# A hybrid S5 / DeltaNet / attention block: the S5 output matrices of layer 0 made by DVE instead of GpSimd

## The chip, the cores and the metric

The kernel runs on one core of a Trainium2 chip. The metric is the device time in microseconds (us). Before the change the median of 3 runs is 2810.09 us (2808.03 to 2811.47). The engines are named as the profile names them: PE is TensorE (its weight loads are PEld), DVE is VectorE, ACT is ScalarE, POOL is GpSimd, and SP issues DMAs.

## The reference, cut to what matters

Two layers, 512 latent tokens and 256 context tokens of width 1024. Each layer normalises the tokens with adaLN shift and scale, multiplies them by one wide input projection `w_in`, runs three mixers side by side (a bidirectional S5 state space model, a chunked gated DeltaNet, windowed attention), merges them and ends with an MLP.

```
h   = rmsnorm(x, norm1_g) * (1 + sc1) + sh1          # sc1, sh1 = silu(c) @ w_mod + b_mod
u, dq, dk, dv, ..., aq, ak, av, gates = split(h @ w_in)
# S5, for each of two directions, 32 groups of 64 complex states:
s_t = a * s_{t-1} + bb @ u_t                         # a, bb from lam, log_dt, b
y_t = Re(c @ s_t) + d * u_t
```

The kernel works the S5 recurrence in chunks of eight tokens. For that it needs, per group and direction, the input matrices `bb * a^k` and the output matrices `c * a^k`, all complex. These products of powers are called tables here. They depend on weights alone, not on the tokens, and are made anew in every launch.

## The kernel before, in words

The program is written for a scheduler that puts each engine's instructions into an order of its own (from a modelled timeline). The order within an engine is then fixed: each engine works its queue strictly from the front, and waits there for what an instruction needs.

The first 350 us hold this work of layer 0:

- **adaLN.** 16 blocks of `w_mod` stream in (L250, issued by SP), PE multiplies them (L254), ACT copies (L257), PE turns the result (L260), DVE reduces and adds (L262, L264). The last L264 writes the last part of the modulation vector `modv`, the shift.
- **Norms.** DVE squares the tokens (L330), PE sums them, a few small steps on DVE and POOL (L345, L347) give the reciprocal root, and DVE multiplies it in (L380, tiles `ntl` for latent and `ntc` for context tokens, eight of each). The shift is added twice: ACT writes `hhi` (L389), the high part of the result, and DVE writes `hlo` (L390), the remainder. Both need the last `modv`.
- **Input projection.** For each weight block, ACT casts the high part `wh` (L230) and DVE makes the remainder `wl` (L231). PE multiplies in L180, over eight steps k, each three products (`hhi,wh`, `hlo,wh`, `hhi,wl`), 512 columns for latent and 256 for context tokens.
- **S5 tables** (`s5_tables`, L538). Layer 0 takes 4 rounds q of 4 group columns (NP=4); the round's two directions d follow one another. For each, DVE makes `tB` (L469 to L474) and from it `tX`, the input matrices. The output matrices `tC` are made from `tcc` and its negative `tcn` (L584 to L587). Both go through `cprod`:

```
u = [pool.tile([128, NP, 8, 16], F32, name=f"tu{nm}{i}", tag=f"tu{tg}{i}", bufs=1)[:, :, :n] for i in range(4)]
for k, (a, i) in enumerate(((src, 0), (src, 1), (src2, 1), (src2, 0))):
    v.tensor_tensor(u[k], a[:, i]..., pb[k % 2], op=OP.mult)      # L563, four
v.tensor_tensor(store(0), u[0], u[1], op=OP.subtract)             # L564
v.tensor_tensor(store(1), u[2], u[3], op=OP.add)                  # L565
```

  Here `v` is the engine, `tg` is "p" for POOL and "v" for DVE, and n is 7 for `tX` (448 columns an instruction) and 8 for `tC` (512 columns). Before, `v` is DVE for `tX` and POOL for `tC`. PE transposes `tX` (L599), ACT copies the result (L601), and it goes to memory in one DMA; PE multiplies `tC` by the padded `tB` (L609, tile `tz`) for the matrices `thx` (L616 to L620). `tC` goes to memory in four DMAs (L591).
- **S5 scan and rope.** On DVE, the scan of the chunk states (L729 to L732) stands between the steps of the rotary embedding for attention (L808, L810, L811, L852), whose result PE needs in L874.

From about 400 us on (DeltaNet, gates, merge, MLP, layer 1) the work is not touched. The tables of layer 1 are made by DVE already, one group column a round (NP=1, so 128 columns an instruction), in the MLP of layer 0.

The tables are a generator that other code drains: one step before the norms, four (`T0A = 4`) after the norms' statistics, which is all four rounds. So in program order all tables of layer 0 are written ahead of the gain and the shift; the scheduler spreads them from there.

Of the kernel before, what the change touches and what calls it, by code (L numbers as in the profile page):

```python
# [183 lines left out]
def setup(g):  # L184
    tc, nc, A = g.tc, g.nc, g.A
    es = g.es
    g.base = es.enter_context(tc.tile_pool(name="base", bufs=1))
    g.wp = es.enter_context(tc.tile_pool(name="wp", bufs=2))
    g.ps = es.enter_context(tc.tile_pool(name="ps", bufs=1, space=PSUM))
    g.dr = es.enter_context(tc.tile_pool(name="dr", bufs=1, space=DRAM))  # L190
    g.ca = g.base.tile([128, CA_N], F32, name="ca")
    nc.sync.dma_start(g.ca, A["ca"])
    g.sm = g.base.tile([128, SM_N], F32, name="sm")
    nc.sync.dma_start(g.sm, A["small"])
    g.ident = g.ca[:, CA_ID:CA_ID + 128]
    g.ones = g.base.tile([128, 32], F32, name="ones")
    nc.gpsimd.memset(g.ones, 1.0)
    g.cneg = g.base.tile([128, 1], F32, name="cneg")
    nc.gpsimd.memset(g.cneg, -0.5)
    g.cpos = g.base.tile([128, 1], F32, name="cpos")  # L200
    nc.gpsimd.memset(g.cpos, 0.5)
    g.hpi = g.base.tile([128, 1], F32, name="hpi")
    nc.gpsimd.memset(g.hpi, math.pi / 2)
    g.modv = g.base.tile([128, NL, 48, 2], F32, name="modv")
    nc.gpsimd.memset(g.modv[:, 1, :, 1], 0.0)
    g.g1 = g.base.tile([128, 8, 2], F32, name="g1a")
    g.g2 = g.base.tile([128, 8, 2], F32, name="g2a")
# [27 lines left out]
def cond_setup(g):  # L235
    nc = g.nc
    c = g.p5a[1].tile([128, 8, NCH], F32, name="cond", tag="uy", bufs=2)[:, :, :32]
    nc.sync.dma_start(c, g.A["cond"])
    g.cs = g.base.tile([128, 8, 32], F32, name="conds")
    nc.scalar.activation(g.cs, c, AF.Tanh, scale=0.5)  # L240
    nc.vector.scalar_tensor_tensor(g.cs, g.cs, 1.0, c, op0=OP.add, op1=OP.mult)


def adaln(g, l, nbs, pool, bufs=2):
    nc = g.nc
    for nb in nbs:
        ps = pm(g, "s")
        for kp in range(4):
            w = pool.tile([128, 1024], F32, name="wa", tag="wa", bufs=bufs)
            g.ad_last = nc.sync.dma_start(w, g.A["wmod"][nb, kp])  # L250
            for k2 in range(2):
                kt = kp * 2 + k2
                c = kt % 4
                nc.tensor.matmul(ps[32 * c:32 * c + 32, :], lhsT=g.cs[:, kt, :], rhs=w[:, k2 * 512:k2 * 512 + 512],  # L254
                                 start=kt < 4, stop=kt >= 4, tile_position=(0, 32 * c))
        ms = pool.tile([128, 512], F32, name="ms", tag="ms", bufs=1)
        nc.scalar.mul(ms, ps, 0.5)  # L257
        p2 = pm(g, "s")
        for j in range(4):
            nc.tensor.transpose(p2[:, j * 128:j * 128 + 128], ms[:, j * 128:j * 128 + 128], g.ident)  # L260
        md = pool.tile([128, 4, 2], F32, name="md", tag="md", bufs=1)
        nc.vector.tensor_reduce(md, raw(p2, 0, [[128, 4], [1, 2], [32, 4]]), axis=AX.X, op=OP.add)  # L262
        bm = g.sm[:, SM_BM + 48 * l + nb * 4:SM_BM + 48 * l + nb * 4 + 4]
        nc.vector.tensor_tensor(g.modv[:, l, nb * 4:nb * 4 + 4, :], md,  # L264
                                bm[:, :, None].to_broadcast([128, 4, 2]), op=OP.add)
        yield
# [22 lines left out]
def drain(it, n=1):  # L289
    for _ in range(n):  # L290
        next(it, None)


def norm_gain(g, l, which):
    dst = g.g1 if which == 0 else g.g2
    gg = g.sm[:, (SM_G1 if which == 0 else SM_G2) + 8 * l:][:, :8]
    sc = g.modv[:, l, 8 + 24 * which:16 + 24 * which, :]
    g.nc.vector.scalar_tensor_tensor(dst, sc, 1.0, gg[:, :, None].to_broadcast([128, 8, 2]), op0=OP.add, op1=OP.mult)
    return dst, g.modv[:, l, 24 * which:24 * which + 8, :]
# [76 lines left out]
def norm_t(g, pool, p, gain, pb, ks=range(8), tag="nt", bufs=2):  # L376
    ts = []
    for k in ks:
        t = pool.tile([128, p.n if bufs > 4 else 512], F32, name=tag, tag=tag, bufs=bufs)[:, :p.n]
        g.nc.vector.scalar_tensor_tensor(t, g.x[:, k, p.sl], gain[:, k, p.r:p.r + 1], pb, op0=OP.mult, op1=OP.mult)  # L380
        ts.append(t)
    return ts
# [10 lines left out]
def norm_apply(g, pool, p, gain, shift, pb, bufs=2):  # L393
    for k in range(8):
        norm_h(g, p, shift, norm_t(g, pool, p, gain, pb, [k], bufs=bufs), [k])
# [35 lines left out]
def new_h(g):  # L431
    p = g.tc.tile_pool(name="h", bufs=1, side="right", reuse_waits="tile")
    pool = p.__enter__()
    t = [pool.tile([128, 8, TOK], F32R, name=nm) for nm in ("hhi", "hlo")]
    g.hv = {s: [x[:, :, off:off + n] for x in t] for s, (n, off) in STREAMS.items()}
    return p, t


def new_hs(g, s):
    p = g.tc.tile_pool(name="h" + s, bufs=1, side="right", reuse_waits="tile")  # L440
    pool = p.__enter__()
    g.hv[s] = [pool.tile([128, 8, STREAMS[s][0]], F32R, name=nm + s) for nm in ("hhi", "hlo")]
    return p
# [906 lines left out]
def s5a_open(g, l):  # L1350
    p = g.tc.tile_pool(name=f"s5a{l}", bufs=1, reuse_waits="tile")
    g.p5a = p, p.__enter__()
# [166 lines left out]
            p.__exit__(None, None, None)  # L1519


T0P = [('c', 0), ('c', 1)]
T0A = 4
AD0 = 7
AD1 = 3
# [283 lines left out]
@with_exitstack  # L1809
def hybrid_block(ctx, tc, A, out):  # L1810
    nc = tc.nc
    g = Ctx()
    g.tc, g.nc, g.A, g.es = tc, nc, A, ctx
    g.tb, g.hd, g.rside, g.pbs, g.plan, g.ldp, g.hst = {}, {}, "right", [], [], [], []
    setup(g)
    s5a_open(g, 0)
    cond_setup(g)
    g.rside = "left"
    tb0 = g.tb0 = s5_tables(g, 0, lambda k, d: nc.gpsimd if (k, d) in T0P else nc.vector, 4, "m")
    drain(tb0)  # L1820
    g.px_ = tc.tile_pool(name="x_in", bufs=1, reuse_waits="tile")
    g.px = g.px_.__enter__()
    g.x = g.px.tile([128, 8, TOK], F32, name="x")
    n1_ = tc.tile_pool(name="n10", bufs=1, reuse_waits="tile")
    n1 = n1_.__enter__()
    sp = s5_params(g)
    drain(sp)
    for k in range(2):
        nc.scalar.dma_start(g.x[:, 4 * k:4 * k + 4, :LAT], A["xT"][:, 4 * k:4 * k + 4, :])
    nc.scalar.dma_start(g.x[:, :, LAT:], A["ctxT"])  # L1830
    drain(sp, 2)
    g.rside = "right"
    with tc.tile_pool(name="ad", bufs=1, side="right", reuse_waits="tile") as pool:
        ad = adaln(g, 0, [2, 3, 0, 1], pool, AD0)
        pbs = []
        for p in P_LC:
            st = Stats(g, n1, p.n, NQ0)
            for k in range(8):
                st.add(k, g.x[:, k, p.sl], k % 2 == 1)
            pbs.append(st.bcast())  # L1840
        drain(tb0, T0A)
        drain(ad, 2)
        gain, shift = norm_gain(g, 0, 0)
        ts = [norm_t(g, n1, p, gain, pb, tag="nt" + p.key, bufs=8) for p, pb in zip(P_LC, pbs)]
        drain(ad, 2)
        g.ldp.append([3, g.ad_last.ins])
    xsd = g.dr.tile([128, 8, TOK], F32, name="xsd", tag="xsd")
    for l in range(NL):
        if l:
            gain, shift = norm_gain(g, l, 0)  # L1850
        if l < NL - 1:
            hp = new_h(g)
        else:
            pa_ = tc.tile_pool(name=f"at{l}", bufs=1, side="right", reuse_waits="tile")
            g.pa = pa_.__enter__()
            hl_ = new_hs(g, "l")
            fl_ = tc.tile_pool(name=f"fl{l}", bufs=1, side="right", reuse_waits="tile")
            g.fl = fl_.__enter__()
            hp = (pa_, hl_, fl_, new_hs(g, "c"))
        if l == 0:  # L1860
            for p, t in zip(P_LC, ts):
                norm_h(g, p, shift, t)
            n1_.__exit__(None, None, None)
        else:
            with tc.tile_pool(name=f"n1{l}", bufs=1, reuse_waits="tile") as pool:
                for p, pb in zip(P_LC, g.pbs):
                    norm_apply(g, pool, p, gain, shift, pb, 4)
                nc.sync.dma_start(xsd[:, :, :LAT], g.x[:, :, :LAT])
        g.px_.__exit__(None, None, None)
        mixers(g, l, hp)  # L1870
        if l == 0:
            merge(g, l, lambda p: A["xT"] if p.key == "l" else A["ctxT"])
        else:
            merge(g, l, lambda p: xsd[:, :, p.sl])
        mlp(g, l, out)
    g.px_.__exit__(None, None, None)
# [17 lines left out]
```

## Time and profile before

| | us |
|---|---|
| median of 3 runs | 2810.09 (2808.03 to 2811.47) |
| the profiled execution | 2808.68 |
| its span on the core | 2806.9 |
| busy: PE | 2642.2 (94%) |
| busy: DVE | 1643.6 (59%) |
| busy: ACT | 871.0 (31%) |
| busy: POOL | 402.5 (14%) |
| mean granted TensorE clock | 0.96 |

The profile is one execution, so its times are read against 2808.68, which lies 1.4 us under the median of the runs. A row of a timeline gives an instruction's start and its duration, or those of a run of like instructions (x4). DVE's instructions overlap a little: the next one starts some 0.07 us before the one ahead is marked as ended, so a run is shorter than the sum of its durations. In square brackets stands how long the engine had been idle and who released it. Busy time is not work at full speed: an instruction that is held up by something the profile doesn't show counts as busy.

### The profile page before, as it was taken

The page shows a single profiled execution, that of the slowest core. Times are in us where ns is not written, and L with a number is a line of the kernel's source. Part 1 is how long each engine was busy: PE and PEld are TensorE (multiplying, and loading weights), DVE is VectorE, ACT ScalarE, POOL GpSimd, SP SyncE. Part 2 cuts the span into 40 slices and gives each one's busy share as a digit, 9 for nine tenths or more (in the row PEclk, how much of TensorE's full clock was granted, in tenths as well). Part 3 has the DMA queues.
Part 4 walks back from the last instruction along what each step waited for, and adds up shares of the span by engine and source line. Part 5 has one row for each costly group of instructions (what it writes and reads, how often), then busy time and mean ns, then how long its engine had stood idle before and what let it go on. Part 6 is the DMA issues. An engine that isn't in the chain of part 4 may idle for free. (4 is left out here: it accounts for less than half of the span.)

```text
span 2806.9 us, 45417 instructions
## 1 busy us (share of the span) xinstructions
PE 2642.2 (94%) x17644; PEld 2171.5 (77%) x17644; DVE 1643.6 (59%) x4100; ACT 871.0 (31%) x1594; POOL 402.5 (14%) x689
## 2 busy tenths in 40 slices
PE   5699899999999899999999999999998999999998
PEld 1576688878777788778888887877776778989997
DVE  7858853237335664999943334896575387434443
ACT  2343342233222333213221223433342234323332
POOL 4600121031112321000000010001231142100001
PEclk8799997699999999999999999999997999999999
DMA  7666322125315441567422115335333246223222
GB/s 235 175 221 232 116 73 76 63 105 162 80 41 171 139 167 53 169 210 229 108 87 65 63 63 167 111 99 178 124 113 84 90 130 202 64 91 98 95 93 68
DMA packets 206760, 344.62 MB, mean 123 GB/s; under 512 B 89296, under 2 KB 121168, under 8 KB 206416
## 3 DMA queue, kind: packets, MB, share of 16 engines
q1 hardware_dynamic: 171856, 298.61, 33.4%
q0 software_dynamic: 9600, 36.71, 3.9%
q10 hardware_dynamic: 25088, 6.40, 1.0%
q8 instruction: 139, 2.28, 0.3%
q14 instruction: 77, 0.63, 0.1%
HBM read 270.09 MB, written 68.16 MB: 121 GB/s over the span
## 5 line engine op out<-in xcount | busy, mean ns | idle before, releaser
L231 DVE TENSOR_TENSOR wl<-ws,wh 128x1024 fp32r<-128x1024 f32 x272 | 340.7, 1254 | 299.5 <-ACT wh L230 286.9
L230 ACT CAST wh<-ws 128x1024 fp32r<-128x1024 f32 x272 | 285.1, 1049 | 668.5 <-PE pg L180 529.9
L180 PE MATMUL pg<-hhil,wh 128*128 128x512 f32 x720 | 292.6, 407 | 10.6 <-ACT cxp L943 7.2
L180 PE MATMUL pg<-hh,wh 128*128 128x512 f32 (+1 forms) x832 | 287.2, 347 | 6.5 <-DVE x L1723 3.0
L180 PE MATMUL pg<-hhil,wl 128*128 128x512 f32 x720 | 289.6, 403 | 2.6 <-DVE wl L231 2.6
L180 PE MATMUL pg<-hlol,wh 128*128 128x512 f32 x720 | 289.7, 403 | 0.0
L180 PE MATMUL pg<-hh,wl 128*128 128x512 f32 (+1 forms) x832 | 285.9, 344 | 1.0 <-DVE wl L231 1.0
L180 PE MATMUL pg<-hl,wh 128*128 128x512 f32 (+1 forms) x832 | 286.6, 345 | 0.0
L180 PE MATMUL pg<-hhi,wh 128*128 128x256 f32 (+1 forms) x800 | 278.4, 348 | 2.7 <-ACT arf L807 1.5
L180 PE MATMUL pg<-hlo,wh 128*128 128x256 f32 (+1 forms) x800 | 277.8, 347 | 1.7 <-DVE hlo L390 1.7
L180 PE MATMUL pg<-hhi,wl 128*128 128x256 f32 (+1 forms) x800 | 276.1, 345 | 0.0
L180 PEld LDWEIGHTS pg<-hh,wh 128*128 128x128 f32 x832 | 158.5, 191 | 29.3 <-issue 6.7
L1723 DVE SCALAR_TENSOR_TENSOR x<-pg,modv,x 128x512 f32<-128x512 f32 (+1 forms) x104 | 64.7, 625 | 197.0 <-PE pg L180 196.7
L180 PEld LDWEIGHTS pg<-hhi,wh 128*128 128x128 f32 x800 | 152.5, 191 | 34.0 <-issue 12.4
L180 PEld LDWEIGHTS pg<-hh,wl 128*128 128x128 f32 x832 | 158.9, 191 | 23.9 <-issue 3.3
L180 PEld LDWEIGHTS pg<-hlo,wh 128*128 128x128 f32 x800 | 152.1, 190 | 30.4 <-issue 11.4
L180 PEld LDWEIGHTS pg<-hl,wh 128*128 128x128 f32 x832 | 158.9, 191 | 21.5 <-issue 4.3
L180 PEld LDWEIGHTS pg<-hhil,wh 128*128 128x128 f32 x720 | 137.5, 191 | 44.9 <-ACT cxp L943 8.2
L180 PEld LDWEIGHTS pg<-hhi,wl 128*128 128x128 f32 x800 | 152.3, 190 | 24.2 <-issue 8.3
L180 PEld LDWEIGHTS pg<-hhil,wl 128*128 128x128 f32 x720 | 137.2, 191 | 38.8 <-DVE wl L231 3.9
L180 PEld LDWEIGHTS pg<-hlol,wh 128*128 128x128 f32 x720 | 137.5, 191 | 33.2 <-issue 3.9
L1626 PE MATMUL pg<-yh,wh 128*128 128x512 f32 (+1 forms) x288 | 105.2, 366 | 11.0 <-DVE macc L1629 6.1
(460 smaller groups left out, 5683.9 us busy)
## 6 DMA issues: line engine op xcount, KB each, us to landing
ws<-in_wt SPq DMA_DIRECT2D x272, 512.0 KB, 3.6
wa<-in_wmod SPq DMA_DIRECT2D x48, 512.0 KB, 4.4
wa<-in_wmodt SPq DMA_DIRECT2D x48, 512.0 KB, 4.4
gtd<-gr POOLq DMA_DIRECT2D x24, 384.0 KB, 2.9
tg<-gtd POOLq DMA_DIRECT2D x24, 384.0 KB, 3.4
tb<-tC SPq DMA_DIRECT2D x64, 128.0 KB, 2.8
cvd<-ctp SPq DMA_DIRECT2D x20, 384.0 KB, 2.6
gtd<-gr POOLq DMA_DIRECT2D x24, 256.0 KB, 2.6
```

The costliest lines, as they stand in the source:

```text
L180: g.nc.tensor.matmul(ps, lhsT=wt[:, a], rhs=x(k), start=i == 0, stop=i == n - 1)
L230: nc.scalar.copy(hi, s)
L231: nc.vector.tensor_tensor(lo, s, hi.bitcast(F32), op=OP.subtract)
L1626: nc.tensor.matmul(ps, lhsT=wt[:, a], rhs=x[:, k, sl], start=i == 0, stop=i == 11)
L1723: g.nc.vector.scalar_tensor_tensor(g.x[:, m, sl], acc, g.modv[:, l, 40 + m, p.r:p.r + 1], g.x[:, m, sl], op0=OP.mult, op1=OP.add)
```

## The change

For layer 0, the engine that makes the output matrices is DVE, as it is for the input matrices. The table of exceptions `T0P` is gone (so the lines behind it are numbered one lower).

```
-T0P = [('c', 0), ('c', 1)]
 T0A = 4
...
-    tb0 = g.tb0 = s5_tables(g, 0, lambda k, d: nc.gpsimd if (k, d) in T0P else nc.vector, 4, "m")
+    tb0 = g.tb0 = s5_tables(g, 0, lambda k, d: nc.vector, 4, "m")
```

Per round and direction this moves one TENSOR_SCALAR of 128 columns, two copies of 64 and six TENSOR_TENSORs of 512 columns, over four rounds and two directions 8, 16 and 48 instructions. Since `tg` is now "v" for both, the four scratch tiles `tuc` share the buffers of `tux`: a product of the one must have been read before the other is written, all on DVE.

The scheduler gives all engines another order in this part of the program. On DVE, the piece ahead of the last shift (the last L264 of adaLN; `tX_465` and `tC_466` belong to round 1, direction 0, `tC_370` to round 0, direction 1):

```order
 L264 TENSOR_TENSOR modv<-md,sm 128x8
+L586 COPY tC_466<-tcc 128x4x16
+L564 TENSOR_TENSOR tC_370<-tuc_403,tuc_404 128x4x8x16
+L565 TENSOR_TENSOR tC_370<-tuc_405,tuc_406 128x4x8x16
+L584 TENSOR_SCALAR tcn<-tcc 128x128
+L262 TENSOR_REDUCE md<-ps 128x8
+L563 TENSOR_TENSOR tux_483<-tB,apw 128x4x112
+L563 TENSOR_TENSOR tux_484<-tB,apw 128x4x112
+L563 TENSOR_TENSOR tux_485<-tB,apw 128x4x112
+L563 TENSOR_TENSOR tux_486<-tB,apw 128x4x112
+L587 COPY tC_466<-tcn 128x4x16
+L264 TENSOR_TENSOR modv<-md,sm 128x8
```

Ten rows now stand between the earlier `modv` and the last one: five for output matrices (L586, L564, L565, L584, L587), the reduction L262, and the four products of `tX_465`.

On PE, before, at the first products of the input projection (L180; L599 transposes tables of round 1):

```order
L609 MATMUL pm<-tC_322,tz_95 32x128 x8
L609 MATMUL pm<-tC_370,tz_96 32x128 x8
L260 MATMUL ps<-ca,ms 128x128 x4
L599 MATMUL pm<-ca,tX_465 128x128 x8
L599 MATMUL pm<-ca,tX_513 128x128 x8
L180 MATMUL pg<-hhi,wh 128x512
L180 MATMUL pg<-hlo,wh 128x512
```

and now, in the same place:

```order
L609 MATMUL pm<-tC_322,tz_95 32x128 x8
L609 MATMUL pm<-tC_370,tz_96 32x128 x8
L599 MATMUL pm<-ca,tX_465 128x128 x3
L180 MATMUL pg<-hhi,wh 128x512
L599 MATMUL pm<-ca,tX_465 128x128 x5
L180 MATMUL pg<-hlo,wh 128x512
L180 MATMUL pg<-hhi,wl 128x512
```

The first product now stands behind three transposes of `tX_465`; those of `tX_513` have gone behind the products of the second 512-column weight block, and L260, the last of adaLN, ahead of the piece.

On DVE, before, around the input matrices `tX_657` of round 2, direction 1:

```order
L472 TENSOR_TENSOR cm_761<-tbb,sf 128x64
L564 TENSOR_TENSOR tX_657<-tux_675,tux_676 128x4x7x16
L643 COPY us<-pg 128x8x32
L565 TENSOR_TENSOR tX_657<-tux_677,tux_678 128x4x7x16
L473 TENSOR_TENSOR tB<-cm_758,cm_759 128x64
L474 TENSOR_TENSOR tB<-cm_760,cm_761 128x64
L231 TENSOR_TENSOR wl<-ws,wh 128x1024
```

and now:

```order
L587 COPY tC_658<-tcn 128x4x16
L643 COPY us<-pg 128x8x32
L564 TENSOR_TENSOR tX_657<-tux_675,tux_676 128x4x7x16
L231 TENSOR_TENSOR wl<-ws,wh 128x1024
L565 TENSOR_TENSOR tX_657<-tux_677,tux_678 128x4x7x16
L473 TENSOR_TENSOR tB<-cm_758,cm_759 128x64
L474 TENSOR_TENSOR tB<-cm_760,cm_761 128x64
```

The remainder `wl` of a weight (L231) now stands between the two halves of `tX_657`, and the products of `tC_658` follow.

## Rows read from the trace of the kernel before

**Rows 1.** Busy time by stretch: us, engine busy (x instructions), PEclk, DMA share, GB/s.
```profile
40.00:140.00 100.00, 62.76 (x423) 44.23 (x423) 91.42 (x149) 33.01 (x75) 72.02 (x70) 0.78 0.63 190
140.00:200.00 60.00, 58.60 (x517) 48.73 (x516) 27.71 (x70) 26.94 (x69) 2.22 (x10) 1.00 0.69 213
200.00:300.00 100.00, 99.89 (x560) 69.06 (x559) 86.81 (x196) 35.31 (x51) 1.54 (x27) 1.00 0.66 228
300.00:345.00 45.00, 35.16 (x213) 28.39 (x212) 41.75 (x85) 12.60 (x19) 5.54 (x5) 0.94 0.29 96
```

**Rows 2.** Timeline of PE, 30 to 124: start, us, engine, line, operation, [idle before].
```profile
61.62 1.05 PE L254 MATMUL ps<-wa,conds 128*32 128x512 f32 x4
...
85.12 2.55 PE L599 MATMUL pm<-ca,tX 128*128 128x128 f32 x10 [10.26 <-DVE modv L264]
87.33 0.78 PE L180 MATMUL pg<-hhi,wh 128*128 128x512 f32 x1
...
116.75 1.11 PE L599 MATMUL pm<-ca,tX 128*128 128x128 f32 x4 [9.03 <-DVE tX L565]
...
121.86 1.08 PE L609 MATMUL pm<-tC,tz 128*32 128x128 f32 x32
```

**Rows 3.** Timeline of DVE, 29 to 135.
```profile
31.42 0.27 DVE L473 TENSOR_TENSOR apw<-cm,cm 128x64 f32<-128x64 f32 x1
...
40.88 4.44 DVE L563 TENSOR_TENSOR tux<-tB,apw 128x448 f32<-128x448 f32 x4
...
51.09 2.21 DVE L563 TENSOR_TENSOR tux<-tB,apw 128x448 f32<-128x448 f32 x4
...
84.55 0.21 DVE L471 TENSOR_TENSOR cm<-tbb,sf 128x64 f32<-128x64 f32 x1
84.69 0.21 DVE L472 TENSOR_TENSOR cm<-tbb,sf 128x64 f32<-128x64 f32 x1
...
84.90 0.15 DVE L264 TENSOR_TENSOR modv<-md,sm 128x8 f32<-128x8 f32 x1
...
92.73 2.72 DVE L390 SCALAR_TENSOR_TENSOR hlo<-ntl,modv,hhi 128x512 fp32r<-128x512 f32 x4
...
106.83 9.87 DVE L565 TENSOR_TENSOR tX<-tux,tux 128x448 f32<-128x448 f32 x1
```

**Rows 4.** Timeline of POOL, beside the last row of Rows 3.
```profile
107.41 2.06 POOL L563 TENSOR_TENSOR tuc<-tcn,apw 128x512 f32<-128x512 f32 x2
...
114.15 2.06 POOL L563 TENSOR_TENSOR tuc<-tcn,apw 128x512 f32<-128x512 f32 x2
```

**Rows 5.** Groups by line, 20 to 140: busy us, mean ns | idle before.
```profile
L563 POOL TENSOR_TENSOR tuc<-tcc,apw 128x512 f32<-128x512 f32 x16 | 20.3, 1286 | 0.0
L563 POOL TENSOR_TENSOR tuc<-tcn,apw 128x512 f32<-128x512 f32 x16 | 18.0, 1139 | 0.0
L565 POOL TENSOR_TENSOR tC<-tuc,tuc 128x512 f32<-128x512 f32 x8 | 13.3, 1660 | 0.0
L564 POOL TENSOR_TENSOR tC<-tuc,tuc 128x512 f32<-128x512 f32 x8 | 10.7, 1336 | 0.0
...
L563 DVE TENSOR_TENSOR tux<-tB,apw 128x448 f32<-128x448 f32 x32 | 26.2, 873 | 0.0
```

**Rows 6.** Instructions of tile tuc: ns min/median/max, first and last start.
```profile
L563 DVE TENSOR_TENSOR tuc<-tcc,apw x64: 269/282/293, 1129.1 to 1422.7; 128x128 f32<-128x128 f32 x64
```

**Rows 7.** Line L180 alone in two stretches: us, PE and PEld busy, PEclk.
```profile
98.90:101.50 2.60, 2.60 (x24) 2.60 (x23) 1.00 0.40 132
118.10:120.40 2.30, 2.30 (x12) 2.30 (x11) 0.50 0.57 91
```

**Rows 8.** Waits from 290 to 350: us in total, times, longest.
```profile
PE pm L874 <- DMA aq<-arf: 7.0, 2, 4.7
```

**Rows 9.** Last DVE row of the scan (timeline), and line L755's instructions.
```profile
340.14 0.27 DVE L732 TENSOR_TENSOR st<-scs 128x112 f32<-128x112 f32 x1
...
L755 PE MATMUL ps<-u,mt x64: 243/421/529, 446.3 to 544.3; 128*128 128x96 f32 x64
```

## The prediction

> **What bounds the kernel now.** I read the busy time by stretch first. From 140 us on PE is the bound: 58.60 of 60 us, then 99.89 of 100 [rows 1]. What reaches PE earlier there ends earlier. From 40 to 140 us it is another engine: PE is busy for 62.76 us, DVE for 91.42, POOL for 72.02, and the tables of layer 0 lie in just this stretch. Second, the timeline of PE: its two longest waits in the stretch both name DVE. It stands for 10.26 us until the last shift (`modv`), and the first product of the input projection (L180) starts at 87.33; it stands for another 9.03 us until `tX`, the second half of one input matrix [rows 2].
>
> Third, the timeline of DVE itself, to see what it does in that time. It does the same thing at very different speeds. Four `tux` products of 448 columns take 2.21 us at 51.09, and 4.44 us at 40.88; one L565, of the same size, takes 9.87 us at 106.83 [rows 3]. Fourth, POOL's timeline: while the 9.87 us row stands, POOL works its output matrices without a gap, from the row at 107.41 to the one that ends at 116.21 (114.15 + 2.06), and DVE's row ends 0.49 us later [rows 3, 4]. At 51.09, where DVE is quick, POOL has no row. So a DVE row with POOL busy beside it is long, and DVE, which bounds this stretch, is partly waiting in rows that count as busy. The 32 `tux` products have a mean of 873 ns [rows 5], against 0.55 us each in the quick run (2.21 / 4) [rows 3].
>
> **The work that changes engine.** From POOL go 48 products of 512 columns: 20.3 + 18.0 + 13.3 + 10.7 = 62.3 us [rows 5], with the small copies about 77. POOL's end sets no term below, so I count nothing for its relief itself. On DVE the same operation with 128 columns takes 0.282 us [rows 6], and one with 448 columns in the quick run starts (2.21 - 0.61) / 3 = 0.53 us after the one before, 0.61 being a row's own length. The straight line through 128 and 448 columns gives a row of 0.68 us at 512, and a start 0.60 us after the last. So 48 x 0.60 = 29 us; at the least 48 x 0.53 = 26, at the most, if every row stayed as long as the stretched ones (4.44 / 4 = 1.11), 53. The 24 small ones (8 negations, 16 copies) are not shown alone on DVE: between nothing and 0.14 us for a copy (the 64-column rows at 84.55 and 84.69 start so far apart [rows 3]) and 0.28 for a negation, 0 to 4.5 in all; I take 3. DVE gets 32 us more work, and loses what the stretching costs it. I sum that over its rows from 20 to 140 at about 42 us: the `tux` products alone (873 - 550) x 32 = 10, the one 9.87 row 9.3, and the rest in the other table rows and in L231. In all DVE should need 7 to 10 us less, not more.
>
> **Term A, the first product.** What counts is where the rows stand in the new order. From the L473 at 31.42 to the end of the last shift DVE now has 110 instructions. At quick spacings: 16 products of 448 columns (8.5), 12 of 512 (7.2), 8 and 8 norm steps L380 of 512 and 256 columns at 0.66 and 0.40 (8.5; spacing as in the four L390 of 2.72 us), 2 remainders of 1024 (2.3), 9 products of 256 (3.0), 6 of 128 (1.2), 30 of 64 (4.0), the rest 1.8: 36.5 us. So the last shift ends at 31.4 + 36.5 = 68.0, where before it ended at 85.05 [rows 3]. Below that it cannot come by more than a few us: the last L254 of adaLN ends at 62.67 [rows 2], and a copy, L260, and two small DVE steps stand behind it, about 65. DVE's queue decides. Behind the shift, 26 rows (11.3 us) stand up to the last latent `hlo`, four products of output matrices among them, so it ends at 79.3; before, at 92.73 + 2.72 = 95.45 [rows 3]. A = -16.1 us. The first L180 should start near 69 or 70.
>
> **Term B, the stall in the third round.** The 9.87 us row goes to about 0.6, and PE's wait of 9.03 us behind it goes [rows 2, 3]. By the new order `tX_657` is done at 106.5, some 10 us before, while PE comes to it earlier by A too; but PE's transposes of it now stand behind more products, and on DVE a `wl` stands inside it. I take the whole 9.0; the bounds are 0 and 9.0.
>
> **Term C, the clock.** After that wait PE's granted clock is 0.50, its lower level of 1.2 GHz, for 12 products in 2.30 us, against 24 in 2.60 us at 2.4 GHz [rows 7]: 0.19 against 0.11 us each. Over the 19 that ran low this is 1.5 to 1.8. C = -1.7; the bounds are -1.7 and 0, as a smaller wait may still end in the low level.
>
> **What comes late next.** In round 1, L609 waits for `tC_514`, now the last table row of its round on DVE, at 91.7, while PE is there at about 90.2: +1.5 (0 to 4). From 300 to 345 us DVE is busy for 41.75 of 45, and PE waits 7.0 us in L874 for the rope's result [rows 1, 8]. There the scheduler has put more rows of the scan between the rope's steps and attention, 13.5 us in place of 9.1 between L808 and L885: +2 (0 to 4.4). That the scan's end comes later relative to PE costs nothing: it ends at 340.14, and its reader starts at 446.3 [rows 9]. That POOL was free to work beside DVE is lost as a cover, but the tables now end on DVE at about 132, about where they ended before.
>
> Sum: -16.1 - 9.0 - 1.7 + 1.5 + 2 = -23.3 us. The profiled execution took 2808.7, so 2785.4; it lies 1.4 under the median of the runs, so the forecast for a median is **2787 us**.
>
> **A rule against the trace.** The 9.87 us row outlasts at least seven POOL rows, each 1.0 to 1.3 us. The Trainium skill, page "SBUF — State Buffer", section "Who interferes with whom", says that a DVE instruction with two SBUF inputs contends with a GpSimd instruction that reads SBUF, and that whoever issues first holds the shared port pair for its whole instruction. The stretching agrees. But taken strictly a DVE row would wait for one POOL instruction, some 1.3 us, and not through seven; by that rule alone 8 of the 9 us of B would have another cause, and B would be near -1. That is the third rival below.
>
> **The rivals.**
>
> - *The gain is given back before 345 us.* If DVE holds PE in the rope's stretch whatever came before, PE ends there no earlier. For it: DVE's 41.75 of 45 us. Against it: from 140 to 345 DVE idles 32.3 + 13.2 + 3.3 = 48.8 us [rows 1], of which the forecast uses 25. It would leave 0 to 5 us: 2804 to 2812, chance 0.09.
> - *Long rows are not POOL's doing.* If DVE's rows are long for a reason of their own (the DMAs that write beside them, the access pattern), they stay long, and DVE only gets more work. The place is the queue ahead of the last shift: 8.2 us of output matrices stand there now, and 3.6 inside the `hlo` steps; the shift comes later by 8.2 and the last `hlo` by 11.8. With B gone from reordering alone it is +3, with B kept +12: 2812 to 2822. It decides from the point where the mean of DVE's `tuc` row stays over about 0.95 us. For it: POOL's own rows vary too (means of 1139 and 1286 ns for the same form [rows 5]). Against it: the quick run at 51.09 with no POOL row, and the end of the 9.87 us row beside POOL's. Chance 0.09.
> - *Only the front.* The shift comes at 68 to 70, but another wait takes the place of B: a table on DVE that PE reaches too soon, since PE is now ahead by 16 us and DVE's queue holds the output matrices between the input matrices. Then A + 0 to 2: about 2793 to 2800. Chance 0.20.
> - *More than the terms.* In the first three rounds DVE is no bound anywhere, and the wait of 7.0 us in L874 shrinks too, since DVE has 7 to 10 us less to do: 2787 - 1.5 - 2 - 7 to -12, so 2765 to 2777. Chance 0.12.
>
> **How the numbers follow.** The forecast, 2780 to 2793, has 0.50. Faster by over 0.2% (5.6 us, about what a measurement can tell from no change) are it, the third and the fourth rival: 0.82. The first rival lies mostly within 0.2%: 0.09 the same. The second is slower: 0.09. The range of 8 in 10 takes the forecast with its bounds (B and C at nothing and both late terms at their ends give 2808.7 - 16.1 + 4 + 4.4 + 1.4 = 2802), part of the first rival and most of the fourth: 2768 to 2807.
>
> **What would show it.** Right: DVE's `tuc` rows of 512 columns near 0.68 us and the 448-column `tux` at 0.61, none of `tX` over 0.8; the last shift's row ending at 67 to 70, the first L180 at 69 to 71, the last latent `hlo` at 78 to 81; no wait of PE over 4 us for `tX`; POOL under 8 us busy from 40 to 140. B is wrong if a wait of 5 us or more for a table stands between 75 and 135. The late terms show in L874's wait, 7 to 12 us. The whole reading is wrong if `tux` rows of 448 columns keep a mean over 0.8 us, or the first L180 starts after 80.

## The result, and the profile after

The changed kernel takes 2779.78 us (median; 2777.29 to 2781.52, 4 runs), the kernel before in the same comparison 2809.06. The ratio is 0.9895, with an interval of 0.9883 to 0.9907: 29 us faster. Two more comparisons gave 0.9891 and 0.9889. The forecast was 2787, in a band of 2780 to 2793, the range 2768 to 2807. The profiled execution has a span of 2779.7 against 2806.9: 27.2 us less.

Busy time by stretch, after, as in [rows 1]:

```profile
40.00:140.00 100.00, 85.79 (x548) 64.71 (x547) 98.71 (x236) 42.37 (x89) 4.97 (x7) 0.86 0.77 236
140.00:200.00 60.00, 59.44 (x546) 49.00 (x545) 38.47 (x89) 30.88 (x75) 1.04 (x17) 1.00 0.63 196
...
300.00:345.00 45.00, 39.69 (x234) 34.14 (x233) 43.45 (x104) 16.85 (x31) 9.94 (x15) 0.96 0.31 87
```

From 40 to 140 us POOL falls from 72.02 to 4.97, and PE rises from 62.76 to 85.79. DVE is no less busy than before, 98.71 in place of 91.42. Its rows by line, 20 to 140, tell that it now works in that time instead of waiting:

```profile
L563 DVE TENSOR_TENSOR tux<-tB,apw 128x448 f32<-128x448 f32 x32 | 18.0, 615 | 0.0
L563 DVE TENSOR_TENSOR tuc<-tcc,apw 128x512 f32<-128x512 f32 x16 | 10.3, 681 | 0.0
...
L565 DVE TENSOR_TENSOR tX<-tux,tux 128x448 f32<-128x448 f32 x8 | 4.9, 615 | 0.0
```

The mean `tux` product falls from 873 [rows 5] to 615 ns, and the output products take 681, where the line through [rows 3, 6] said 0.68 us. Timeline of DVE, after:

```profile
39.85 0.43 DVE L330 TENSOR_TENSOR nsq<-x 128x256 f32<-128x256 f32 x1 [4.08 <-PE pm L309]
...
72.79 0.15 DVE L264 TENSOR_TENSOR modv<-md,sm 128x8 f32<-128x8 f32 x1
...
83.46 0.74 DVE L390 SCALAR_TENSOR_TENSOR hlo<-ntl,modv,hhi 128x512 fp32r<-128x512 f32 x1
...
110.86 0.61 DVE L565 TENSOR_TENSOR tX<-tux,tux 128x448 f32<-128x448 f32 x1
```

The row that took 9.87 us [rows 3] takes 0.61. Its readers on PE, after (L599 of `tX_657`, which before waited 9.03 us [rows 2]), have no wait:

```profile
114.34 0.60 PE L599 MATMUL pm<-ca,tX 128*128 128x128 f32 x4
...
115.26 0.60 PE L599 MATMUL pm<-ca,tX 128*128 128x128 f32 x4
```

At the front, timeline of PE and POOL, after:

```profile
36.70 2.08 PE L350 MATMUL pm<-ca,nr 128*128 128x128 f32 x8 [5.41 <-POOL nr L347]
...
69.85 1.26 PE L609 MATMUL pm<-tC,tz 128*32 128x128 f32 x16 [5.20 <-DVE tC L564]
...
74.30 0.78 PE L180 MATMUL pg<-hhi,wh 128*128 128x512 f32 x1
```

```profile
31.20 5.45 POOL L347 TENSOR_TENSOR nr<-nv,cneg 128x4 f32<-128x4 f32 x1 [29.66 <-DVE nv L345]
50.41 1.78 POOL L347 TENSOR_TENSOR nr<-nv,cneg 128x2 f32<-128x2 f32 x1 [13.76 <-DVE nv L345]
```

The first product comes at 74.30 in place of 87.33, but the forecast was 69 to 70. The last shift ends at 72.94 and the last latent `hlo` at 84.20, 4.9 us later than forecast each. The row of DVE at 39.85 shows where these are lost: DVE idles 4.08 us for PE, and PE stands 5.41 us (L350, at 36.70) for POOL's L347, which takes 5.45 us for 4 columns.

**Where the 27 us come from.** The two kernels are set against each other up to PE's first L874 (340.0 and 312.9). Before:

```profile
0.00:40.00 40.00, 18.60 (x70) 5.65 (x70) 22.28 (x100) 9.22 (x18) 10.28 (x20) 0.96 0.72 244
40.00:87.30 47.30, 20.91 (x131) 9.99 (x131) 47.30 (x81) 11.38 (x26) 38.52 (x35) 0.70 0.57 182
87.30:124.00 36.70, 25.97 (x185) 21.79 (x184) 34.10 (x54) 15.78 (x38) 21.48 (x23) 0.78 0.54 147
124.00:200.00 76.00, 74.47 (x626) 61.17 (x626) 37.73 (x86) 32.78 (x81) 14.25 (x23) 1.00 0.76 234
...
300.00:340.00 40.00, 32.48 (x204) 25.97 (x202) 39.53 (x77) 11.72 (x17) 5.02 (x4) 0.99 0.22 70
sum 340.00, PE 272.32 PEld 193.63 DVE 267.75 ACT 116.20 POOL 91.08; mean PE 45.39 PEld 32.27 DVE 44.62 ACT 19.37 POOL 15.18
```

After, cut at the same places of the program as near as the order allows:

```profile
0.00:40.00 40.00, 15.65 (x52) 4.80 (x52) 18.89 (x96) 7.24 (x13) 6.45 (x12) 0.93 0.68 228
40.00:74.30 34.30, 21.04 (x138) 9.68 (x136) 33.34 (x90) 13.59 (x30) 1.78 (x1) 0.70 0.71 242
74.30:98.90 24.60, 23.66 (x146) 19.38 (x144) 24.60 (x57) 12.44 (x27) 1.47 (x2) 0.84 0.65 182
98.90:172.90 74.00, 73.44 (x574) 63.19 (x572) 59.21 (x142) 33.05 (x75) 2.43 (x15) 1.00 0.81 246
...
272.90:312.90 40.00, 36.39 (x222) 25.48 (x220) 35.63 (x87) 11.33 (x16) 3.36 (x4) 1.00 0.38 129
sum 312.90, PE 270.17 PEld 192.82 DVE 253.56 ACT 117.07 POOL 16.84; mean PE 45.03 PEld 32.14 DVE 42.26 ACT 19.51 POOL 2.81
```

The PE column gives the idle time as the stretch less the busy time. Up to 40 us it rises from 21.4 to 24.4 (+3.0); from there to the first product it falls from 26.4 to 13.3 (-13.1); over the next stretch, with the stall, from 10.7 to 0.9 (-9.8); then from 1.5 to 0.6 (-1.0); in the last 40 from 7.5 to 3.6 (-3.9). With -0.1 in the full stretch between, that is -24.95. PE's busy time falls by 2.15, from 272.32 to 270.17. The two make up the 27.1 us. The 2.15 is a balance: L180 takes 1.1 us less, with 24 of its products started at the lower clock before and 13 now, but PE's busy time at that clock is 22.1 and 22.2 us in all, since rows ahead of the first product (L350, part of L609) now fall into it. Behind the first L874 both profiles take the same time, 2466.9 and 2466.8 us.

### The profile page after: what moved, and what is told of

Its sections match the earlier page's. It is cut to its first block, busy times and chain, and to the rows that moved or that the text cites. A ratio compares the mean times of both kernels' runs of the same rounds, so it can differ in the third digit from the quotient of the medians.

```text
span 2779.7 us, 45405 instructions
## 1 busy us (share of the span) xinstructions
PE 2640.6 (95%) x17644; PEld 2173.9 (78%) x17644; DVE 1639.4 (59%) x4172; ACT 873.0 (31%) x1594; POOL 331.0 (12%) x617
## 5 line engine op out<-in xcount | busy, mean ns | idle before, releaser
L231 DVE TENSOR_TENSOR wl<-ws,wh 128x1024 fp32r<-128x1024 f32 x272 | 340.2, 1252 | 309.2 <-ACT wh L230 297.8
L180 PE MATMUL pg<-hhil,wh 128*128 128x512 f32 x720 | 291.3, 405 | 11.0 <-ACT cxp L943 7.4
L180 PE MATMUL pg<-hh,wh 128*128 128x512 f32 (+1 forms) x832 | 287.3, 347 | 6.6 <-DVE x L1722 4.0
L180 PE MATMUL pg<-hhil,wl 128*128 128x512 f32 x720 | 289.6, 402 | 2.0 <-DVE wl L231 2.0
L180 PE MATMUL pg<-hlol,wh 128*128 128x512 f32 x720 | 288.3, 401 | 0.0
L180 PE MATMUL pg<-hh,wl 128*128 128x512 f32 (+1 forms) x832 | 285.5, 344 | 1.0 <-DVE wl L231 1.0
L180 PE MATMUL pg<-hl,wh 128*128 128x512 f32 (+1 forms) x832 | 286.1, 345 | 0.0
L180 PE MATMUL pg<-hhi,wh 128*128 128x256 f32 (+1 forms) x800 | 277.6, 348 | 2.2 <-ACT gr L1429 2.0
L180 PE MATMUL pg<-hlo,wh 128*128 128x512 f32 (+1 forms) x800 | 277.7, 347 | 0.9 <-DVE hlo L390 0.9
L180 PE MATMUL pg<-hhi,wl 128*128 128x512 f32 (+1 forms) x800 | 276.3, 346 | 0.0
L180 PEld LDWEIGHTS pg<-hh,wh 128*128 128x128 f32 x832 | 158.5, 191 | 29.5 <-DVE x L1722 4.6
L180 PEld LDWEIGHTS pg<-hh,wl 128*128 128x128 f32 x832 | 158.8, 191 | 23.9 <-issue 3.3
L180 PEld LDWEIGHTS pg<-hlo,wh 128*128 128x128 f32 x800 | 151.9, 190 | 30.9 <-issue 12.6
L180 PEld LDWEIGHTS pg<-hhi,wh 128*128 128x128 f32 x800 | 152.3, 191 | 29.6 <-issue 7.0
L180 PEld LDWEIGHTS pg<-hl,wh 128*128 128x128 f32 x832 | 158.8, 191 | 21.1 <-issue 4.1
L180 PEld LDWEIGHTS pg<-hhi,wl 128*128 128x128 f32 x800 | 151.9, 190 | 26.3 <-issue 9.8
L180 PEld LDWEIGHTS pg<-hhil,wh 128*128 128x128 f32 x720 | 137.1, 191 | 44.5 <-ACT cxp L943 8.2
L180 PEld LDWEIGHTS pg<-hhil,wl 128*128 128x128 f32 x720 | 136.7, 190 | 37.9 <-issue 3.8
L180 PEld LDWEIGHTS pg<-hlol,wh 128*128 128x128 f32 x720 | 137.1, 190 | 31.2 <-issue 2.1
```

Source lines behind the costliest of these rows:

```text
L180: g.nc.tensor.matmul(ps, lhsT=wt[:, a], rhs=x(k), start=i == 0, stop=i == n - 1)
L231: nc.vector.tensor_tensor(lo, s, hi.bitcast(F32), op=OP.subtract)
```

## The experiments

### Does GpSimd hold DVE up, or did the new order do it?

Three kernels add GpSimd work to the changed kernel, behind the second `nr`, on a tile that nobody else uses. PE, DVE, ACT and SP have the same queues in all three, row for row; only what GpSimd does differs. These queues are not those of the changed kernel, so the three are compared with one another.

```
 drain(tb0, T0A)
+memset(dm[:, 1]); copy(dm[:, 0, :2], nr)
+pool_read:  48 x tensor_tensor(dm[:, 0], dm[:, 1], dm[:, 1], mult)
+pool_write: 100 x memset(dm[:, 0], 1.0)
+pool_mix:   24 x (tensor_tensor as above, then 2 memsets)
```

Expected of the products:

> The changed kernel, with 48 GpSimd products of 512 columns added behind the second nr (from about 52 us), that read and write a tile of their own which nobody else uses. No instruction of another engine waits for them, but the queues differ a little from the changed kernel's behind round 1. Theory A, GpSimd rows that read SBUF hold up DVE's rows with two SBUF inputs: the 448-column tux rows go from 0.61 us back to a mean of 0.8 to 1.1, single rows over 2 us come back, and in proportion to the 77 us of GpSimd work in the kernel before (42 us of stretching) some 55 us of it give 30 us on DVE, 20 to 28 at the end: 2798 to 2808. Theory B, the gain came from the new order of the queues alone: tux stays at 0.61 us and the whole at 2778 to 2784.

Of the memsets:

> As the run with 48 added GpSimd products, but with 100 memsets of 512 columns in their place (about 50 us of GpSimd, from about 52 us on), which write SBUF and read nothing. The queues of PE, DVE, ACT and SP are the same in both, row for row. Theory A1, what holds DVE up is that GpSimd reads: tux stays at 0.61 us, and the whole at 2778 to 2784. Theory A2, any busy GpSimd holds DVE up: as with the products, 2798 to 2808.

Of the mixture, written when the first two were known:

> As the runs with 48 added GpSimd products (2832.8) and with 100 added memsets (2801.4), with the same queues on PE, DVE, ACT and SP, row for row: here 24 products, each with two memsets behind it, so that GpSimd is as busy and reads half as often. Theory 1, each GpSimd row that reads costs DVE the same: half of the 31.4 us between the two, 2815 to 2819, tux at a mean of 0.70 to 0.76 us. Theory 2, DVE gets its rows in while GpSimd writes and the price of a reading row falls: 2803 to 2810.

| | median us | ratio to before |
|---|---|---|
| 100 memsets | 2801.43 | 0.9973 [0.9960, 0.9985] |
| 24 products, 48 memsets | 2815.29 | 1.0023 [1.0011, 1.0036] |
| 48 products | 2832.80 | 1.0087 [1.0071, 1.0103] |

With memsets, `tux` on DVE, and busy time from 40 to 140 us (the fifth is POOL):

```profile
L563 DVE TENSOR_TENSOR tux<-tB,apw 128x448 f32<-128x448 f32 x32 | 17.9, 618 | 0.0
```

```profile
40.00:140.00 100.00, 79.98 (x524) 59.96 (x524) 96.28 (x240) 37.59 (x79) 59.08 (x110) 0.83 0.77 235
```

GpSimd is busy for 59.08 of the 100 us, and `tux` is no longer for it (615 ns in the changed kernel). Copies, which have one input, are: nearly 0.2 us alone, a few of them take 0.3 to 0.6 beside a memset.

```profile
67.40 0.51 DVE L587 COPY tC<-tcn 128x64 f32<-128x64 f32 x1
```

With products, `tux` and the first part of GpSimd's run:

```profile
L563 DVE TENSOR_TENSOR tux<-tB,apw 128x448 f32<-128x448 f32 x24 | 19.2, 854 | 0.0
```

```profile
48.59 43.12 POOL L1840 TENSOR_TENSOR dm<-dm 128x512 f32<-128x512 f32 x29
```

The rows of both are longer: 854 ns on DVE, and GpSimd's products 1.49 us on average in this run, against 1.03 in [rows 4]. With half of them, 715 ns:

```profile
L563 DVE TENSOR_TENSOR tux<-tB,apw 128x448 f32<-128x448 f32 x32 | 21.1, 715 | 0.0
```

So it is GpSimd's reading that holds these rows up, not that it is busy: 48 products cost 31.4 us, 24 cost 13.9, about 0.6 us each, nearly in proportion. DVE's rows tell the same. Each row from 20 to 200 us less the median of its form in the changed kernel gives, added up, 4.6 us with memsets, 16.9 with the mixture and 33.7 with products; it is 35.3 in the kernel before and 1.7 in the changed one. Theory A, A1, and theory 1 of the mixture stand. The size for the products was too low: 2833 where 2798 to 2808 was expected, partly because the memsets alone stood at 2801 and not at 2780, which none of the theories foresaw. The section after the next one looks for the cause of that in the order.

### The row of 9.87 us

Taken strictly, the rule that the prediction quotes gave a DVE row at most one GpSimd row to wait for, and the prediction named its third rival there. The kernel before was profiled again, and the added products were made to write three tiles in turn:

```
-tensor_tensor(dm[:, 0], dm[:, 1], dm[:, 1], mult)
+tensor_tensor(dm[:, (0, 2, 3)[i % 3]], dm[:, 1], dm[:, 1], mult)
```

> The kernel before once more, for a second profile of it. The question is the one row of 9.87 us (L565 of tX, DVE). Theory 1, GpSimd keeps DVE out through a whole run of its rows whenever the two meet in this place: the row is there again, 8 to 11 us long, with GpSimd rows back to back beside it, and PE waits 8 to 10 us behind it. Theory 2, it was an accident of that one execution (some other delay): the row is under 3 us, and L874 is reached 8 us sooner than in the first profile, while the whole stays near 2809.

> As the run with 48 added GpSimd products that all write one tile, one behind the other, but here they take three tiles in turn, so that no product has to wait until the one ahead has written. The queues of PE, DVE, ACT and SP are the same in both, row for row. The products reading and writing the same tile let DVE in after each row: no DVE row there is over 1.7 us. Theory 1, DVE gets in after every GpSimd row in any case: DVE's rows as in that run, GpSimd's at 1.5 to 1.6 us, the whole at 2830 to 2836. Theory 2, GpSimd rows that need not wait for one another keep DVE out through a run of them, as beside the row of 9.87 us: GpSimd's rows at 1.05 us, DVE rows of 4 us and more, the whole at 2835 to 2860.

The second profile of before (2804.87 us, one run) has the row again, 9.87 us long, in the same place:

```profile
106.66 0.41 DVE L643 COPY us<-pg 128x256 f32<-128x256 f32 x1
107.00 9.87 DVE L565 TENSOR_TENSOR tX<-tux,tux 128x448 f32<-128x448 f32 x1
```

PE waits 9.07 us behind it. It is no accident. With three tiles the whole is 2830.37 us (2 runs), and DVE still gets in after every product, two rows in 2.97 us; GpSimd has 33 rows in 40.74, 1.23 each, where theory 1 had 1.5 to 1.6:

```profile
64.63 2.97 DVE L563 TENSOR_TENSOR tuc<-tcc,apw 128x512 f32<-128x512 f32 x2
67.52 2.97 DVE L563 TENSOR_TENSOR tuc<-tcn,apw 128x512 f32<-128x512 f32 x2
```

```profile
48.85 40.74 POOL L1840 TENSOR_TENSOR dm<-dm 128x512 f32<-128x512 f32 x33
```

So the products' independence is not what lets GpSimd keep DVE out, and theory 2 falls. That GpSimd's run makes the 9.87 us row rests on the two profiles, where the row ends 0.49 us after the run; no other kernel reproduced it. Other rows show the same in the opposite direction. In the mixture one GpSimd product takes 6.04 us, beside two DVE rows of L231 at their usual 1.2 us, four products and four small rows behind them:

```profile
57.57 1.10 POOL L1840 MEMSET dm<- 128x512 f32 x2
58.76 6.04 POOL L1840 TENSOR_TENSOR dm<-dm 128x512 f32<-128x512 f32 x1
```

```profile
58.59 2.35 DVE L231 TENSOR_TENSOR wl<-ws,wh 128x1024 fp32r<-128x1024 f32 x2
```

The Trainium skill ("SBUF — State Buffer", section "Who interferes with whom") says that a DVE instruction with two SBUF inputs contends with a GpSimd instruction that reads SBUF and not with one that only writes; the memsets and the products show just that. It also says (section "SBUF: two separate sides") that the one that starts first holds the shared ports for its whole instruction. Most rows agree (about one neighbour's length more), but 9.87 and 6.04 us are several instructions long, so one side can wait through a run of the other's. When it alternates and when it runs is not settled here.

### Half of the change

```
-T0P = [('c', 0), ('c', 1)]
+T0P = [('c', 1)]
```

> Half of the change: of the output matrices of layer 0, DVE makes those of direction 0, GpSimd still those of direction 1 (24 products in place of 48). Theory A (contention), stretching in proportion to GpSimd's reading: about half of the gain, 2790 to 2798, with tux at a mean of 0.70 to 0.78 us. Rival (a balance would be best, since GpSimd's free time takes half the load off DVE): 2774 or less.

Measured: 2805.78, ratio 0.9998 [0.9986, 1.0011]. No gain at all, and both theories missed. `tux` is as slow as before with half of GpSimd's work (before: 873 ns):

```profile
L563 DVE TENSOR_TENSOR tux<-tB,apw 128x448 f32<-128x448 f32 x32 | 26.4, 885 | 0.0
```

`tux` alone misleads here. Over all DVE rows from 20 to 200 us, added up as above, the stretching is 20.3 us against 35.3 before: it has nearly halved, as theory A had it, and the time has not followed. To see why, the kernels are compared at PE's first L874, which has the same products ahead of it in all of them. Half the change reaches it at 338.7 us, before at 340.0, the changed kernel at 312.9:

```profile
0.00:338.70 338.70, 278.88 (x1766) 197.47 (x1767) 266.06 (x624) 116.29 (x228) 62.43 (x94) 0.92 0.62 198
```

PE's idle time is 59.8 us there, against 67.7 before, but its busy time is 278.9 against 272.3, with 36 us of it at the lower clock against 22. So the waits fall by 7.8 us and 6.6 of that are given back by products that run slower. Against the changed kernel it loses 17.1 us to waits and 8.7 to busy time. Most of these waits are in L685, the first products of the S5 scan, whose operand goes to memory and comes back by DMA:

```profile
150.52 2.83 PE L685 MATMUL ps<-u,om 128*64 128x96 f32 x32 [6.65 <-DMA om<-tb]
...
160.90 1.55 PE L685 MATMUL ps<-u,om 128*64 128x96 f32 x16 [3.43 <-DMA om<-tb]
```

These are 10.1 us. The scheduler has put the first L685 behind 268 products of L180; in the changed kernel it stands behind 359 and waits 0.6 us at the most. Before it stands behind 229 and waits 1.4 us, so the place alone doesn't decide: the matrices must also come early enough. In the kernel with the 100 memsets it stands behind 262:

```profile
139.52 1.54 PE L685 MATMUL ps<-u,om 128*64 128x96 f32 x32 [1.63 <-DMA om<-tb]
...
149.01 1.55 PE L685 MATMUL ps<-u,om 128*64 128x96 f32 x16 [4.50 <-DMA om<-tb]
```

That kernel reaches L874 at 327.5 us, 14.6 behind the changed kernel, with `tux` as short as there: 11.2 us of waits, 5.6 of them in L685 and 2.9 in L874, and 3.4 of busy time. So the order can cost more than 10 us by itself, as far as the rows show; no run isolates it. The medians lie 24 us apart, of which this profile shows 14. Every change to this source re-orders all queues, and such a wait may come or go with it.

### GpSimd's first row

> The changed kernel once more, as the measure for the runs beside it. Every theory: about 2780 us, 0.985 to 0.993 of the kernel before.

> The changed kernel with one more GpSimd instruction near 1 us: a power of 4 columns into a tile that nobody reads. The queues of the other four engines are the same, row for row. In the changed kernel the first L347 (nr) takes 5.45 us, in the kernel before 2.34 behind other GpSimd work. Theory 1, the first arithmetic instruction on GpSimd costs some 3 us more, and the change has made L347 the first: here nr takes 2.0 to 2.5 us, DVE's idle time of 4.08 us before L330 falls under 1, the last shift comes at about 69.5 in place of 72.8, and the whole is 2776 to 2778. Theory 2, nr is long because DVE's rows hold it off: nr stays at 5 us or more, the last shift at 72.8, and the whole at 2780.

```
 nc.gpsimd.memset(g.cpos, 0.5)
+wrm = g.base.tile([128, 4], F32, name="wrm")
+nc.gpsimd.tensor_tensor(wrm, g.cpos..., g.cneg..., op=OP.pow)     # pad: nc.gpsimd.memset(wrm, 0.5)
```

The changed kernel again took 2777.16. In this second profile, L347 takes 1.16 us, as the first arithmetic row on GpSimd all the same:

```profile
31.58 1.16 POOL L347 TENSOR_TENSOR nr<-nv,cneg 128x4 f32<-128x4 f32 x1 [30.05 <-DVE nv L345]
```

So there is no price of a first use, and theory 1 falls. Theory 2 asked for 5 us or more each time, and that falls too: the same queues gave 5.45, 1.16 and, in a third profile, 1.16 for the first `nr` and 4.09 for the second. With the early power it took 1.23 and 2.75, with the tile alone 5.44. With a short `nr`, DVE and PE are where the prediction put them:

```profile
67.98 0.15 DVE L264 TENSOR_TENSOR modv<-md,sm 128x8 f32<-128x8 f32 x1
...
78.83 0.75 DVE L390 SCALAR_TENSOR_TENSOR hlo<-ntl,modv,hhi 128x512 fp32r<-128x512 f32 x1
```

```profile
69.49 0.78 PE L180 MATMUL pg<-hhi,wh 128*128 128x512 f32 x1
```

The last shift ends at 68.13 (forecast 68.0), the last latent `hlo` at 79.58 (79.3), the first product starts at 69.49 (69 to 70).

The early power gave 2769.23, 0.9864 [0.9839, 0.9889], lower than the 2776 to 2778 of theory 1. To see whether that was the instruction or its tile:

> The changed kernel with the tile of 4 columns of the run with the early power on GpSimd, but filled by a memset: all queues are those of the changed kernel, but for this one memset, and all later tiles lie 16 bytes a partition higher. That run came out at 2769 in place of 2777, though its first nr row (1.23 us) was no shorter than the changed kernel's in its second profile (1.16). Theory 1, the early arithmetic instruction on GpSimd did it: here 2777 to 2782. Theory 2, the shifted addresses: 2767 to 2772. Theory 3, chance among few runs: in between, and both within 5 us.

> The changed kernel again, as the measure for the run with the early power on GpSimd beside it: 2775 to 2782.

> The changed kernel with the early power on GpSimd again; before it came out at 2769.2 beside 2777.2 of the changed kernel and 2775.5 of the one with the tile alone, all with the same queues. If the early arithmetic instruction does something: 2766 to 2772, 6 us or more under the changed kernel beside it. If it was chance among few runs: within 4 us of it.

The tile alone gave 2775.53, between the bounds as in theory 3, but 6.3 us from 2769.23 where that asked for 5. The changed kernel a third time gave 2778.62, the early power again 2775.97 (0.9874 [0.9859, 0.9889] beside 0.9889 [0.9873, 0.9905]). Intervals overlap. By the second pair, 2.6 us, it is chance by the terms set. The profiles of the first pair say the same. Their spans, 2769.1 and 2780.5, lie 11.4 us apart, but PE reaches L874 at 307.7 and 309.3. The other 9.8 us lie behind it, where both have the same queues (early power, then the changed kernel):

```profile
307.70:2769.10 2461.40, 2366.76 (x15878) 1989.94 (x15878) 1384.23 (x3540) 755.45 (x1366) 313.72 (x559) 0.97 0.36 113
309.30:2780.50 2471.20, 2375.62 (x15878) 1984.76 (x15878) 1383.11 (x3540) 756.13 (x1366) 313.84 (x559) 0.96 0.36 112
```

The granted clock is at its lower level for 167 us in the one and 188 in the other. The early power has the lowest median measured, but it isn't shown to beat the change.

## Why the prediction was right, point by point

- **What bounds the stretch:** DVE, by rows that wait inside their busy time. Right, and shown by memsets against products with the same queues.
- **The moved work:** 48 x 0.60 us. The output rows are 0.68 us long, as the line gave. Right. The stretching was put too high, at 42 us where the rows add up to 35: DVE's busy time over the whole execution fell from 1643.6 to 1639.4 us, 4 less and not 7 to 10.
- **Term A, -16.1.** The last latent `hlo` is 15.9 us earlier in the second profile and 11.3 in the first, where PE's idle time up to the first product fell by 10.1. What failed in the first was the sum of DVE's queue without idle time: 36.5 us of rows, but DVE stood 4.08 us for PE, that for L347, and 0.96 more for L260. So of the signs set for the front, 67 to 70 for the shift, 69 to 71 for L180 and 78 to 81 for `hlo`, the recorded profile missed all three. The prediction said that GpSimd's relief sets no term, and did not count GpSimd's own two rows left on the way to the shift, which DVE can hold up in turn.
- **Terms B and C, -9.0 and -1.7.** PE's idle time in that stretch fell by 9.8. The lower clock behind the stall is gone (PEclk 1.00 from 98.90 on), which is what C stood for; its size can't be read off alone, since the 2.15 us of busy time are a balance. Right. The third rival (only the front) did not come; the rule by which the prediction introduced it doesn't cover the 9.87 us row.
- **The late terms, +1.5 and +2,** had the wrong sign. L609 does not wait for `tC_514`, and PE's wait for the rope fell from 7.0 [rows 8] to 4.7 us (5.6 in the second profile of before, 4.4 in two more of the changed kernel), after:

```profile
PE pm L874 <- DMA aq<-arf: 4.7, 2, 3.6
```

  The last 40 us up to L874 lost 3.9 us of idle time, where the two terms had added 3.5. Of the 3.9 only 1.0 is in that wait; the rest are two others that are gone, 1.3 us in L984 and 1.5 in L180. In the recorded profile this 7.4 and A's miss (6.0 by idle time) have opposite signs, so the sum came within 4 us: -23.3 forecast, -27.1 measured. The likeliest number was right to that extent by two errors that nearly cancel. In the second profile A was met, and PE reached L874 at 309.3, 3.7 us sooner, but the execution was no shorter (a span of 2780.5): the part behind L874 took 4.4 us more.
- **The band, the first rival and the fourth.** 2779.78 lies just under the band of 2780 to 2793, towards the fourth rival (more than the terms), whose sign did come in part: the wait in L874 shrank. That rival's own terms give 2771 to 2777; its 2765 does not follow from them. The first rival (the gain is given back before 345 us) is excluded, with L874 reached 27 us sooner.
- **POOL under 8 us, `tux` under 0.8:** 4.97 and 0.615. A wait for a table of 5.20 us is there, in L609 at 69.85, but ahead of the first product and not in the stretch where it would have told against B.
- **The second rival (long rows are not GpSimd's doing)** is excluded.

## What to carry to other kernels

An engine that is busy in a profile may be waiting inside its rows: compare the same form of instruction with its neighbour busy and idle before counting its work. Taking work off a full engine to GpSimd costs that engine if GpSimd reads SBUF beside instructions with two SBUF inputs: here 62 us of products on GpSimd stretched DVE's rows by some 35 us, and making them itself costs it about 32. The gain is larger than the difference because of where the stretched rows stood: 19.8 us ahead of the last shift and 9.3 in the one row, both in front of a long wait of PE. Where a scheduler orders the queues, test such a cause with kernels whose other queues are the same, since the order seems to have moved the time by more than 10 us here.

## What the runs showed of the hardware that was not expected

GpSimd's writing costs DVE's products with two inputs nothing (59 us of memsets, `tux` at 618 ns), but copies some (0.51 us in place of 0.18); its reading costs about 0.6 us a product at the end. One row can wait for far longer than one neighbour's row: 9.87 us on DVE, in both profiles of before, and 5.45 and 6.04 us on GpSimd. Two of these waits end with the other's unbroken run: the 9.87 us row 0.49 us after GpSimd's, the 5.45 us row 0.87 us after DVE fell idle. The same queues gave a GpSimd row 1.16 or 5.45 us from one execution to the next.
